# A decoder layer's MLP: third tile of right operands from another pool, and a seventh tile for sums

## The chip, the cores and the metric

The kernel runs on one core of one Trainium2 chip. The metric is the device time of one execution in microseconds; before the change the median of three runs is 2434.29 us (2431.82 to 2435.8). The core has five engines, which work at the same time, each through its own list of instructions in a fixed order: PE (TensorE: matmuls, with PEld for its weight loads), DVE (VectorE), ACT (ScalarE), POOL (GpSimd) and SP (SyncE), which here issues the DMAs. An instruction waits until what it reads is written and what it overwrites is no longer needed; everything behind it on the same engine waits with it.

## The reference

One layer of a decoder on 2048 tokens of width 1024: stick-breaking attention in 12 heads beside a cross-attention of 4 heads into 256 memory tokens, one output projection, a layer norm, and an MLP with a squared ReLU and a second layer norm.

```python
proj = x @ w_in_sb[slot]
mix = merge_heads(stick_breaking_attention(q, k, v))
mem_out = memory_attention(q_mem, mem, w_mem_kv[layer])
y = jnp.concatenate([mix, mem_out.astype(mix.dtype)], axis=-1) @ w_out[layer]
x = layer_norm(DN_ALPHA * x + y, ln_mix_g[layer], ln_mix_b[layer])
h = jnp.square(jax.nn.relu(x @ w_up[layer]))
x = layer_norm(DN_ALPHA * x + h @ w_down[layer], ln_ffn_g[layer], ln_ffn_b[layer])
```

All inputs are float32. `w_up` is 1024 x 4096, `w_down` 4096 x 1024.

## The kernel before

Each float32 operand of a matmul is split into two float16 parts, a high part (ACT writes it) and a low part (DVE writes the difference: `split_sb`, lines 713 and 714, for operands in SBUF; `split_ps`, lines 161 and 162, for those in PSUM). A product is three passes over these parts: high by high, high by low, low by high (`PASSES`). The first two passes need the high part of the left factor of `matmul`, `lhsT`, and only the last needs its low part.

The projections and the attention come first, until about 1090 us. Their order on every engine is written out by hand. There `turn` (lines 313 to 319) splits each block of attention weights into a tile of the pool "p2" (ACT line 317, POOL line 318), and SP issues a DMA that transposes it (line 319). A tile of "p2" can be written again when that DMA has read it. The pool has six tiles.

Then comes the MLP, in two halves of 1024 tokens. It multiplies by a scheme of Strassen's kind: seven products of blocks where eight would be needed, on sums and differences of blocks. The 4096 columns of `w_up` are taken in 16 blocks of columns, `fp` = 0 to 15, in pairs (`GROUP` = 2). For one block, `up` (from line 812) makes seven products of 12 matmuls each, in three banks of PSUM, `upa`, `upb` and `upc`: r11 into `upa`, rt2 into `upb`, rt1 into `upc`, r21 into `upa`, rt3 into `upb`, r22 into `upc`, rt4 into `upb`. The banks are read by ACT and DVE in between: `u1` is a copy of `upa` by ACT (line 863), DVE adds it to `upb` (line 866) and to `upc` (line 869), and later lines 874, 876 and 878 add further products. A product that goes into a bank for the second time waits for the instruction that reads the first. Lines 836 to 841 apply the squared ReLU and split the result into seven tiles `hl`, and `sums` (lines 843 to 856) makes four sums of them. After the two blocks of a pair, `down` (from line 891) multiplies the `hl` by the rows of `w_down`, in the tiles `wr`, in banks `dna`, `dnb` and `dnc`, and adds to `acc` (DVE lines 917, 919, 948 and 956, POOL lines 921 and 958). The last pair (`fp` 14 and 15) takes plain products in `down`.

The right operands of one block of `up` are seven split matrices, in four tiles: keys 0 to 2 hold two each (r11 and rt2; rt1 and r21; rt3 and rt4) and key 3 holds r22. In half 0 they are made from `w_up`: SP loads two raw tiles `wu` (line 788, pool "st", three tiles), POOL makes four differences `t` (line 774, in tiles of "p2"), ACT and DVE split, and SP stores the split tiles to DRAM (`keptup`, line 768). The rows of `w_down` go the same way: raw tiles `wd` (line 889, "st"), differences `t_d` (line 774, "p2"), splits into `wr`, stores `keptdown`. In half 1 the stored tiles are loaded again (line 816 for `rt`, line 1135 for `wr`).

Pools are lists of equal tiles under a tag. "X" has 16 tiles of 4 KB per partition. In the MLP eight of them hold `acc` and seven hold `hl`. "ws" has five tiles of 4 KB, "p2" six of 2 KB, "st" three. In the MLP the order of instructions on each engine is set by a scheduler when the kernel is built, from its own estimate of times and from which tile is free when; it is fixed at run time.

Of the kernel before, what the change touches and what calls it, by code (L numbers as in the profile page):

```python
# [10 lines left out]
F16 = mybir.dt.float16  # L11
# [5 lines left out]
P = 128  # L17
# [17 lines left out]
def trunk_layer(ctx: ExitStack, tc: tile.TileContext, x, mem, w_in, w_kv, w_out,  # L35
# [19 lines left out]
    HB = KT // 2  # L55
# [14 lines left out]


    DMA_DIAG = (2, 3)
    BUFS = dict(X=16, g=15, st=3, ws=5, et=7, p2=6, tt=2, pw=4)

    def sbt(tag, shape, dt, name):
        return sb.tile(shape, dt, tag=tag, name=name, bufs=BUFS[tag])

    def pst(tag, name):
        return pools["ps"].tile([P, C], F32, tag=tag, name=name, bufs=pools["bufs"][tag])
# [631 lines left out]
    def split_sb(hi, lo, src, scale):  # L711
        with early():
            A.activation(hi, src, AF.Copy, scale=scale)  # L713
            V.scalar_tensor_tensor(lo, src, scale, hi, ALU.mult, ALU.subtract)  # L714
# [44 lines left out]
    def operand(tiles, s, j, k):  # L759

        return tiles[s][j][:, :, k, :] if isinstance(tiles[s], list) else tiles[s][:, :, j * HB + k, :]
# [3 lines left out]
    def keep(key, t, shape):  # L765

        kept[key] = dr.tile(shape, F16, name="kept" + "_".join(map(str, key)))
        nc.sync.dma_start(kept[key], t)

    def right_sums(b11, b12, b21, b22, view, name):  # L770

        def diff(x, y, n):
            t = view(sbt("p2", [P, C], F32, f"t{n}_{name}"))
            G.tensor_tensor(t, x, y, ALU.subtract)
            return t

        t1 = diff(b12, b11, 1)
        t2 = diff(b22, t1, 2)
        t3 = diff(b22, b12, 3)
        t4 = diff(b21, t2, 4)  # L780
        return t1, t2, t3, t4

    def up_right(fp, nm):

        raw = []
        for i in range(2):
            t = sbt("st", [P, HB, 2 * P], F32, f"wu{nm}_{i}")
            nc.sync.dma_start(t, w_up[i * HB * P:(i + 1) * HB * P, fp * 2 * P:(fp + 1) * 2 * P]
                              .rearrange("(k p) f -> p k f", p=P))
            raw.append(t)  # L790
        b11, b12 = raw[0][:, :, :P], raw[0][:, :, P:]
        b21, b22 = raw[1][:, :, :P], raw[1][:, :, P:]
        t1, t2, t3, t4 = right_sums(b11, b12, b21, b22, lambda t: t.rearrange("p (k f) -> p k f", f=P), nm)

        def right(key, *srcs):
            n = len(srcs)
            t = sbt("ws" if n == 2 else "p2", [P, n, 2, HB, P], F16, f"rt{nm}")
            for i, s in enumerate(srcs):
                split_sb(t[:, i, 0], t[:, i, 1], s, SW)
            keep(("up", fp, key), t, [P, n, 2, HB, P])  # L800
            return [t[:, i] for i in range(n)]

        r11, rt2 = right(0, b11, t2)
        rt1, r21 = right(1, t1, b21)
        rt3, rt4 = right(2, t3, t4)
        r22, = right(3, b22)
        return r11, rt2, rt1, r21, rt3, rt4, r22

    def up(half, fp, ops, hl, wr, g, plain):


        nm = f"{half}_{fp}"
        if half:
            def right(i, n):
                t = sbt("ws" if n == 2 else "p2", [P, n, 2, HB, P], F16, f"rt{nm}")
                nc.sync.dma_start(t, kept["up", fp, i])
                return [t[:, i] for i in range(n)]

            r11, rt2 = right(0, 2)
            rt1, r21 = right(1, 2)  # L820
            rt3, rt4 = right(2, 2)
            r22, = right(3, 1)
        else:
            r11, rt2, rt1, r21, rt3, rt4, r22 = up_right(fp, nm)
        def prod(bank, s, r, start):
            bv = bank.rearrange("p (t n) -> p t n", n=P)
            n = 0
            for a, b in PASSES:
                for k in range(HB):
                    T.matmul(bv, lhsT=r[:, a, k, :], rhs=operand(ops, s, b, k), start=start and n == 0,  # L830
                             stop=n == 3 * HB - 1, skip_group_check=not start)
                    n += 1

        def activate(t, s, src=None):

            A.activation(t, t if src is None else src, AF.Relu, scale=math.sqrt(SH) / (SX * SW))  # L836
            if s is not None:
                A.activation(hl[s][:, g, 0, :], t, AF.Square)
            A.activation(t, t, AF.Square)
            if s is not None:  # L840
                V.tensor_tensor(hl[s][:, g, 1, :], t, hl[s][:, g, 0, :], ALU.subtract)  # L841

        def put(s, t):
            split_sb(hl[s][:, g, 0, :], hl[s][:, g, 1, :], t, 1.0)

        def sums(h11, h12, h21, h22):
            s1 = sbt("et", [P, C], F32, f"s1_{nm}")
            V.tensor_tensor(s1, h21, h22, ALU.add)
            put(S1, s1)
            s2 = sbt("et", [P, C], F32, f"s2_{nm}")  # L850
            V.tensor_tensor(s2, s1, h11, ALU.subtract)
            put(S2, s2)
            V.tensor_tensor(h21, h11, h21, ALU.subtract)
            put(S3, h21)
            V.tensor_tensor(h12, h12, s2, ALU.subtract)
            put(S4, h12)

        ba = pst("bk", f"upa{nm}")
        bb = pst("bk", f"upb{nm}")
        bc = pst("bk", f"upc{nm}")  # L860
        prod(ba, A11, r11, True)
        u1 = sbt("et", [P, C], F32, f"u1_{nm}")
        A.activation(u1, ba, AF.Copy)  # L863
        prod(bb, S2, rt2, True)
        u2 = sbt("et", [P, C], F32, f"u2_{nm}")
        V.tensor_tensor(u2, bb, u1, ALU.add)
        prod(bc, S1, rt1, True)
        u3 = sbt("et", [P, C], F32, f"u3_{nm}")
        V.tensor_tensor(u3, bc, u1, ALU.add)  # L869
        prod(ba, A12, r21, False)  # L870
        h11 = sbt("et", [P, C], F32, f"r_{nm}")
        activate(h11, A11, ba)
        prod(bb, S3, rt3, False)
        V.tensor_tensor(u3, bb, u3, ALU.add)  # L874
        prod(bc, S4, r22, False)
        V.tensor_tensor(u2, bc, u2, ALU.add)
        prod(bb, A22, rt4, False)
        V.tensor_tensor(u1, bb, u1, ALU.add)
        activate(u3, A22)
        activate(u1, A21 if plain else None)  # L880
        activate(u2, A12)
        if not plain:
            sums(h11, u2, u1, u3)
        if half:
            return
        rows = []
        for f in range(2 * fp, 2 * fp + 2):
            t = sbt("st", [P, D], F32, f"wd{nm}_{f}")
            nc.sync.dma_start(t, w_down[f * P:(f + 1) * P, :])
            rows.append(t)  # L890
        b11, b12, b21, b22 = (r[:, n * C:(n + 1) * C] for r in rows for n in range(2))
        ts = (b12,) if plain else right_sums(b11, b12, b21, b22, lambda t: t, "d" + nm)
        for s, t in zip((B11, B21, B22, T1, T2, T3, T4), (b11, b21, b22) + ts):
            split_sb(wr[s][:, g, 0, :], wr[s][:, g, 1, :], t, SD)
            keep(("down", fp, s), wr[s][:, g], [P, 2, C])
# [125 lines left out]
    for c in range(NC):  # L1021
        if c < len(kv_work):
            fn, hp, c0, nm = kv_work[c]
# [100 lines left out]
    for half in range(NC // 2):  # L1124
        if half == 0:
            load_gb(g2, b2, [(gbs[:, 0], gbs[:, 1]), (gbs[:, 2], gbs[:, 3])])
        for f0 in range(0, NFP, GROUP):
# [21 lines left out]
            for n, _ in enumerate(work):  # L1149
                i = n // 2  # L1150
# [38 lines left out]
```

## Time and profile before

| what | us |
|---|---|
| median of three runs | 2434.29 |
| the profiled execution | 2430.05 |
| its span, from first to last instruction | 2428.3 |
| PE busy in the span | 2237.2 |
| DVE busy | 1709.7 |
| ACT busy | 1185.7 |
| POOL busy | 1021.7 |

A row of the timeline gives start, length, engine, source line, operation, what is written, what is read (buffer numbers are left out), and the count of instructions merged into it; square brackets hold the idle time ahead of it and what ended it. A row of the windows gives the stretch, its length and the busy time and count of each engine, then the granted clock of PE as a share of full speed, the share of the DMA engines and GB/s. A row of the chain gives start, length and what the end of the stretch was waiting for at that time. A row of the waits gives who waited for whom, the total, the count and the longest.

### The profile page before, as it was taken

The numbers are of one execution on the slowest core, as the hardware profiler recorded it, in microseconds if no ns is written. First come the engines' busy times: TensorE is split into PE (matmuls) and PEld (weight loads), VectorE is DVE, ScalarE is ACT, GpSimd is POOL, SyncE is SP. The second block draws the span as 40 slices with busy tenths as digits, with TensorE's granted clock in tenths as the row PEclk, the third lists the DMA queues.
The fourth block names the chain that finished last, engine by engine and source line by source line (L and its number), as shares of the span: only waits on it lengthen the run. The fifth ranks groups of instructions, "written<-read, shape, count | busy, mean of one in ns | idle before, by whom it ended". The sixth has DMA issues, their size and how long they took to land.

```text
span 2428.3 us, 34523 instructions
## 1 busy us (share of the span) xinstructions
PE 2237.2 (92%) x12032; PEld 1000.8 (41%) x12032; DVE 1709.7 (70%) x2385; ACT 1185.7 (49%) x2577; POOL 1021.7 (42%) x826
## 2 busy tenths in 40 slices
PE   7798999999989999997799999999997999999996
PEld 4343434344334343333344444444443444444443
DVE  4456777777776777779987888888676454555447
ACT  4456677776766656544544454445433322233321
POOL 0001656566564556564654456443443122211124
PEclk9899999999999999998999999999998999999998
DMA  7244888879887787876643445334565333323211
GB/s 260 44 85 90 154 162 152 162 137 163 150 160 143 165 173 170 167 178 183 220 165 114 142 152 182 133 115 149 169 194 190 105 109 96 108 87 96 96 44 70
DMA packets 606285, 342.03 MB, mean 141 GB/s; under 512 B 487840, under 2 KB 544672, under 8 KB 606112
## 3 DMA queue, kind: packets, MB, share of 16 engines
q1 hardware_dynamic: 606112, 339.84, 55.8%
q8 instruction: 94, 1.54, 0.3%
q14 instruction: 79, 0.65, 0.1%
HBM read 143.65 MB, written 77.59 MB: 91 GB/s over the span
## 4 chain that ended last, share of the span: by engine, by line
PE 58%; DVE 18%; issue 8%; ACT 7%; DMA 5%; POOL 3%; SPq 0%; ACTq 0%; DVEq 0%; POOLq 0%
PE dnb L906 7%; PE upb L830 7%; PE dnc L906 5%; PE dna L906 5%; PE upc L830 5%; PE upa L830 4%; PE pq L252 4%; PE z L280 4%; PE op L670 4%; PE av L340 3%; PE kp L252 3%; PE vp L252 3%; DVE wr L714 2%; DVE e L466 2%; POOL t L318 2%
## 5 line engine op out<-in xcount | busy, mean ns | idle before, releaser
L318 POOL TENSOR_TENSOR t<-e,t 128x512 f16<-128x512 f32 (+1 forms) x384 | 431.6, 1150 | 360.0 <-ACT t L317 293.0
L830 PEld LDWEIGHTS <-rt 128*128 128x128 f16 x2688 | 266.2, 99 | 387.7 <-issue 81.1
L906 PEld LDWEIGHTS <-hl 128*128 128x128 f16 x2736 | 267.4, 98 | 335.5 <-DVE hl L841 11.2
L466 DVE TENSOR_TENSOR_SCAN e<-z,carry,zero 128x512 f32<-128x512 f32 x288 | 350.4, 1265 | 44.5 <-ACT z L458 30.2
L921 POOL TENSOR_TENSOR acc<-acc,v 128x512 f32<-128x512 f32 x112 | 149.9, 1341 | 503.1 <-DVE acc L919 432.4
L458 ACT ACTIVATE z<-z 128x512 f32<-128x512 f32 (+1 forms) x480 | 226.6, 513 | 229.5 <-PE z L280 123.7
L830 PE MATMUL upb<-op,rt 128*128 128x512 f16 x1152 | 269.6, 383 | 13.0 <-DVE u L874 6.9
L906 PE MATMUL dnb<-wr,hl 128*128 128x512 f16 x1008 | 236.1, 380 | 0.0
L317 ACT ACTIVATE t<-e 128x512 f16<-128x512 f32 (+1 forms) x384 | 225.9, 616 | 7.7 <-DMA w<-t 6.9
L280 PE MATMUL z<-k,q 64*128 64x512 f16 (+3 forms) x1440 | 186.0, 349 | 32.3 <-DVE e L466 31.7
L830 PE MATMUL upa<-op,rt 128*128 128x512 f16 x768 | 184.8, 389 | 26.3 <-ACT u L863 19.3
L830 PE MATMUL upc<-op,rt 128*128 128x512 f16 x768 | 183.7, 387 | 16.1 <-DVE u L869 16.1
L670 PE MATMUL op<-wo,mx 128*128 128x512 f16 x720 | 171.6, 387 | 1.8 <-DVE acc L677 1.8
L466 DVE TENSOR_TENSOR_SCAN e<-z,zero 128x128 f32<-128x128 f32 (+1 forms) x192 | 147.0, 806 | 32.1 <-ACT z L458 24.9
L906 PE MATMUL dna<-wr,hl 128*128 128x512 f16 x672 | 155.0, 380 | 9.7 <-DVE hl L841 9.7
L906 PE MATMUL dnc<-wr,hl 128*128 128x512 f16 x672 | 161.1, 379 | 1.8 <-ACT hl L713 1.1
L340 PE MATMUL av<-w,v 128*64 128x512 f16 (+3 forms) x1440 | 145.9, 349 | 4.5 <-DMA w<-t 4.5
L252 PE MATMUL vp<-xT,wv 128*128 128x512 f16 x576 | 140.4, 388 | 0.0
L252 PE MATMUL pq<-xT,wq 128*128 128x512 f16 x576 | 138.7, 385 | 0.0
L252 PE MATMUL kp<-xT,wk 128*128 128x512 f16 x576 | 136.0, 380 | 0.0
L836 ACT ACTIVATE u<-u 128x512 f32<-128x512 f32 x96 | 60.3, 628 | 132.9 <-DVE u L874 78.6
L280 PEld LDWEIGHTS <-q 64*128 64x128 f16 x1440 | 55.4, 94 | 148.7 <-issue 104.7
(177 smaller groups left out, 3248.0 us busy)
## 6 DMA issues: line engine op xcount, KB each, us to landing
keptdown<-wr SPq DMA_DIRECT2D x106, 256.0 KB, 2.5
wr<-keptdown SPq DMA_DIRECT2D x106, 256.0 KB, 2.9
keptup<-rt SPq DMA_DIRECT2D x48, 512.0 KB, 3.0
rt<-keptup SPq DMA_DIRECT2D x48, 512.0 KB, 3.6
wu<-in_w_up_dram SPq DMA_DIRECT2D x32, 512.0 KB, 4.6
wd<-in_w_down_dram SPq DMA_DIRECT2D x32, 512.0 KB, 4.0
x<-in_x_dram SPq DMA_DIRECT2D x16, 512.0 KB, 10.3
acc<-in_x_dram SPq DMA_DIRECT2D x16, 512.0 KB, 5.2
```

The source lines that it names most:

```text
L252: T.matmul(pp, lhsT=wt[:, a, k, :], rhs=xs(xT, c, b, k), start=n == 0, stop=n == 3 * KT - 1)
L280: T.matmul(banks[h], lhsT=q[rows, a, i * P:(i + 1) * P], rhs=keys(b)[rows], start=n == 0, stop=stop and n == 2)
L317: A.activation(hi, src, AF.Copy)
L318: G.tensor_tensor(lo, src, hi, ALU.subtract)
L340: T.matmul(av[h * HD:(h + 1) * HD, i0 * P:].rearrange("p (t n) -> p t n", n=P), lhsT=vv(h, a), rhs=pT(h, b)[:, i0:, :], start=first and n ...
L458: A.activation(t.z[:, :t.W], t.z[:, :t.W], AF.Sigmoid, scale=-SCORE)
L466: V.tensor_tensor_scan(t.e[:, t.W - 1::-1], t.z[:, t.W - 1::-1], zero[:, 0:1].broadcast_to([P, t.W]), init, ALU.mult, ALU.add)
L670: T.matmul(pp, lhsT=lhs, rhs=W[f"o{k}"][:, kb, n * C:(n + 1) * C], start=m == 0, stop=m == 3 * NKO - 1)
L830: T.matmul(bv, lhsT=r[:, a, k, :], rhs=operand(ops, s, b, k), start=start and n == 0, stop=n == 3 * HB - 1, skip_group_check=not start)
L836: A.activation(t, t if src is None else src, AF.Relu, scale=math.sqrt(SH) / (SX * SW))
L906: mm = T.matmul(bank, lhsT=hl[s][:, g, a, i * P:(i + 1) * P], rhs=wr[r][:, g, b, :], start=start and m == 0, stop=m == 3 * n - 1, skip_gro ...
L921: G.tensor_tensor(sl, sl, u, ALU.add)
```

## The change

The tile of key 2 (rt3 and rt4) is no longer taken from "ws" but from "X", in both halves, and "p2" gets a seventh tile. So a block takes two of the five tiles of "ws", not three, and one of "X". No instruction is added or removed.

```diff
-    BUFS = dict(X=16, g=15, st=3, ws=5, et=7, p2=6, tt=2, pw=4)
+    BUFS = dict(X=16, g=15, st=3, ws=5, et=7, p2=7, tt=2, pw=4)
...
         def right(key, *srcs):
             n = len(srcs)
-            t = sbt("ws" if n == 2 else "p2", [P, n, 2, HB, P], F16, f"rt{nm}")
+            t = sbt(("ws", "ws", "X", "p2")[key], [P, n, 2, HB, P], F16, f"rt{nm}")
...
             def right(i, n):
-                t = sbt("ws" if n == 2 else "p2", [P, n, 2, HB, P], F16, f"rt{nm}")
+                t = sbt(("ws", "ws", "X", "p2")[i], [P, n, 2, HB, P], F16, f"rt{nm}")
                 nc.sync.dma_start(t, kept["up", fp, i])
```

In the attention every engine keeps its order. In the MLP the scheduler sets another, the same for each pair of blocks but the first and the last. The three pieces below are from half 0, around blocks 4 and 5; a name like rt_5_14491 is a tile with the number of its block and its own number (14477, 14484, 14491 and 14498 are keys 0 to 3 of block 5).

POOL, beside the `down` of the pair before (L921 and L958 add to `acc`); t_0_5 are the differences for block 5, t_d_4 those for the rows of `w_down`:

```order
 L774 TENSOR_TENSOR t_d_4_14435<-wd_4_9_14427,t_d_4_14431 128x512
 L774 TENSOR_TENSOR t_0_5_14469<-wu_5_0_14465 128x512
+L774 TENSOR_TENSOR t_0_5_14471<-wu_5_1_14467,t_0_5_14469 128x512
 L921 TENSOR_TENSOR acc_9441<-acc_9441,v_0_0_14055 128x512
+L774 TENSOR_TENSOR t_0_5_14473<-wu_5_1_14467,wu_5_0_14465 128x512
 L921 TENSOR_TENSOR acc_9921<-acc_9921,v_0_1_14064 128x512
 L958 TENSOR_TENSOR acc_10616<-acc_10616,v_0_0_14088 128x512
```

Two differences of block 5 move up past eight additions to `acc`.

DVE, in block 4 from the first reading of `upb` (L866) to that of `upc` (L869):

```order
 L866 TENSOR_TENSOR u_0_4_14329<-upb_4_14301,u_0_4_14315 128x512
-L714 SCALAR_TENSOR_TENSOR rt_5_14498<-wu_5_1_14467,rt_5_14498 128x512
-L714 SCALAR_TENSOR_TENSOR rt_5_14491<-t_0_5_14473,rt_5_14491 128x512
-L714 SCALAR_TENSOR_TENSOR rt_5_14491<-t_0_5_14475,rt_5_14491 128x512
+L714 SCALAR_TENSOR_TENSOR rt_6_14926<-wu_6_0_14914,rt_6_14926 128x512
 L714 SCALAR_TENSOR_TENSOR wr_4_3_14258<-t_d_5_14632,wr_4_3_14258 128x512
 L919 TENSOR_TENSOR acc_11077<-acc_11077,dnb_2_14164 128x512
+L714 SCALAR_TENSOR_TENSOR wr_4_4_14259<-t_d_5_14634,wr_4_4_14259 128x512
 L919 TENSOR_TENSOR acc_11286<-acc_11286,dnb_3_14173 128x512
-L714 SCALAR_TENSOR_TENSOR wr_4_4_14259<-t_d_5_14634,wr_4_4_14259 128x512
+L714 SCALAR_TENSOR_TENSOR wr_4_5_14260<-t_d_5_14636,wr_4_5_14260 128x512
+L869 TENSOR_TENSOR u_0_4_14343<-upc_4_14302,u_0_4_14315 128x512
```

L869 stood behind eight instructions after L866 (the eighth, a split of wr_4_6, follows this piece, and L869 after it) and now stands behind six; the splits of key 2 of block 5 have left this place.

ACT, in block 4 from the end of `u2` (L839 on u_0_4_14329) to the copy of block 5's `upa` (L863):

```order
 L839 ACTIVATE u_0_4_14329<-u_0_4_14329 128x512
-L713 ACTIVATE rt_6_14933<-t_0_6_14918 128x512
-L713 ACTIVATE rt_6_14933<-wu_6_1_14916 128x512
+L713 ACTIVATE rt_7_15129<-wu_7_0_15117 128x512
 L836 ACTIVATE u_0_4_14315<-u_0_4_14315 128x512
 L839 ACTIVATE u_0_4_14315<-u_0_4_14315 128x512
-L713 ACTIVATE rt_6_14940<-t_0_6_14922 128x512
-L713 ACTIVATE rt_6_14940<-t_0_6_14924 128x512
 L713 ACTIVATE hl_4_3_14251<-s_0_4_14411 128x512
 L863 ACTIVATE u_0_5_14518<-upa_5_14503 128x512
```

Four splits of block 6 leave this place, and one of block 7, which reads a raw tile two blocks ahead, comes in front of L836. On DVE the same split stands in front of L848, and the splits of key 2 of block 5 now come behind the four sums of block 4, those of block 6 behind the last product of block 5. On SP the load of that raw tile, wu_7_0, stands behind the stores of keys 0 and 3 of block 6 in both kernels.

In half 1 the first load of a key-2 tile after the first, rt_1_18632, stands behind the eight loads of `acc` for the second half, and PE takes the two products of that tile, rt3 and rt4 of block 1, in one row of 24 matmuls behind five products of `down`. In later pairs the load of the odd block's key 2 stands behind the load of key 1 of the block two further.

## Rows read from the trace of the kernel before

**Rows 1.** Windows: attention, one pair of blocks in half 0, half 1.
```profile
225.00:1090.00 865.00, 809.15 (x5195) 342.02 (x5196) 658.62 (x773) 560.89 (x1416) 508.81 (x447) 0.99 0.82 159
1363.00:1442.00 79.00, 73.27 (x338) 32.92 (x337) 66.86 (x85) 37.29 (x65) 39.86 (x28) 1.00 0.42 147
1865.00:2428.00 563.00, 545.04 (x2526) 246.88 (x2524) 297.33 (x484) 159.27 (x262) 131.50 (x102) 0.99 0.29 91
```

**Rows 2.** Waits of PE from 1245 to 1700 us.
```profile
PE upc L830 <- DVE u L869: 15.7, 6, 2.9
PE upb L830 <- DVE u L866: 4.7, 5, 1.0
PE upb L830 <- DVE u L874: 4.7, 3, 1.6
PE upa L830 <- ACT u L863: 3.5, 5, 0.7
```

**Rows 3.** Timeline of PE, one pair of blocks.
```profile
1416.51 0.59 PE L830 MATMUL upa<-op,rt 128*128 128x512 f16 x2
1419.62 2.75 PE L830 MATMUL upc<-op,rt 128*128 128x512 f16 x12 [2.52 <-DVE u L869]
...
1426.31 5.12 PE L830 MATMUL upb<-op,rt 128*128 128x512 f16 x23 [1.57 <-DVE u L874]
...
1436.02 2.75 PE L830 MATMUL upa<-op,rt 128*128 128x512 f16 x12 [0.69 <-ACT u L863]
...
1441.23 2.75 PE L830 MATMUL upb<-op,rt 128*128 128x512 f16 x12 [0.95 <-DVE u L866]
```

**Rows 4.** Timeline of PE, waits in three other places.
```profile
1195.39 4.63 PE L830 MATMUL upa<-op,rt 128*128 128x512 f16 x12 [10.96 <-ACT u L863]
...
1498.52 4.25 PE L830 MATMUL upc<-op,rt 128*128 128x512 f16 x12 [2.52 <-DVE u L869]
...
1656.63 4.41 PE L830 MATMUL upc<-op,rt 128*128 128x512 f16 x12 [2.52 <-DVE u L869]
```

**Rows 5.** Chain of waits from 1395 to 1420 us.
```profile
1397.28 1.75 DVE wr L714 x2
...
1401.04 1.28 POOL t L774
...
1402.34 3.99 DMA wd<-in_w_down_dram
...
1406.88 1.13 ACT wr L713 x2
...
1418.89 0.68 DVE u L869
```

**Rows 6.** Timeline of DVE from 1409 to 1426 us.
```profile
1409.53 0.68 DVE L866 TENSOR_TENSOR u<-upb,u 128x512 f32<-128x512 f32 x1
...
1412.63 1.75 DVE L714 SCALAR_TENSOR_TENSOR wr<-t_d,wr 128x512 f16<-128x512 f32 x1
1414.31 1.27 DVE L919 TENSOR_TENSOR acc<-acc,dnb 128x512 f32<-128x512 f32 x2
1415.50 3.46 DVE L714 SCALAR_TENSOR_TENSOR wr<-t_d,wr 128x512 f16<-128x512 f32 x2
...
1425.58 0.68 DVE L874 TENSOR_TENSOR u<-upb,u 128x512 f32<-128x512 f32 x1
```

**Rows 7.** Instructions on tile u: durations in ns, least, median, most.
```profile
L836 ACT ACTIVATE u<-u x33: 613/630/631, 1287.4 to 1687.5; 128x512 f32<-128x512 f32 x33
...
L848 DVE TENSOR_TENSOR s<-u,u x11: 692/693/1525, 1295.6 to 1688.9; 128x512 f32<-128x512 f32 x11
...
L863 ACT ACTIVATE u<-upa x10: 573/576/580, 1329.0 to 1671.7; 128x512 f32<-128x512 f32 x10
```

**Rows 8.** Loads of wu (line 788): issue of one, and landing.
```profile
L788 SPq DMA_DIRECT2D wu<-in_w_up_dram x32: 383/386/1005, 1090.8 to 1706.7; - x32
...
DMA to landing us min/median/max: 3.9/4.6/5.6
```

**Rows 9.** Loads of rt in half 1 (line 816): landing.
```profile
DMA to landing us min/median/max: 2.5/3.6/10.9
```

**Rows 10.** Waits of ACT in the attention.
```profile
ACT t L317 <- DMA w<-t: 6.9, 8, 2.0
```

## What the change was predicted to do, and why

> **What bounds the kernel now.** I read the busy times by window first, to see which engine fills each part. In half 1 PE is busy 545 of 563 us [rows 1]: nothing that only moves other engines' work can gain much there. In the attention PE is busy 809 of 865 us and the list of instructions stays the same. Half 0 of the MLP is the place to look: a pair of blocks takes 79 us, in which PE works 73 and DVE 67 [rows 1], so PE sets the pace with holes in it.
>
> The waits of PE come next. From 1245 to 1700 us, which is six pairs, it waits 15.7 us for L869, 4.7 for L866, 4.7 for L874 and 3.5 for L863 [rows 2], together 28.6. The timeline of one pair shows where: 2.52, 1.57, 0.69 and 0.95 us, 5.73 in the pair [rows 3]. In three of the later pairs there is no wait for L874, but the 12 matmuls behind the wait for L869 take 4.25 us (first) to 4.41 (last) instead of 2.75 [rows 3, 4]. That is about 1.6 us three times, 4.8 in all. So the repeated loss is 28.6 + 4.8 = 33.4 us over six pairs. The first pair has a hole of its own, 10.96 us at the copy L863 [rows 4].
>
> Why L869 is late is read from the chain of waits: a split of `wr` on DVE frees a tile, POOL makes a difference (1.28), only then can the next raw rows be loaded (3.99), ACT splits (1.13), and the chain ends at 1418.89 with L869 [rows 5]. On DVE the instructions between L866 and L869 are slow ones: a split of two SBUF operands takes 1.75 us there, or 3.46 for two, where one that reads PSUM takes 0.64 to 0.68 [rows 6].
>
> **The change part by part.** Nothing is added or removed, so busy time changes only by what lies beside what. "X" has 8 + 7 of 16 tiles in use, so there is one tile for key 2, and its next use must wait until `up` has read it and its store has gone. "ws" now holds keys 0 and 1 of two and a half blocks instead of all three of one and two thirds.
>
> *Wait for L869.* Two differences of block 5 are made earlier on POOL, so the raw tile is free earlier and the load of `wd` starts earlier. Three splits of key 2 leave the stretch in front of L869 and a single new one comes: six instructions instead of eight. Two DVE splits fewer are worth 1.4 us at 0.68 each (the least row) to 3.5 (the pair in [rows 6]); with the load no longer last, L869 begins at 1418.89 less about 3.3 to 5.4, at 1413.5 to 1415.6. PE is ready at 1416.51 + 0.59 = 1417.10 [rows 3]. The wait of 2.52 goes, and with it the slow matmuls behind it.
>
> *Wait for L874.* With that wait gone PE comes to its next wait at 1426.31 − 1.57 − 2.52 = 1422.2, and L874 ends at 1426.26 now [rows 3, 6]. It would have to come forward by 4.0, and 3.3 to 5.4 is what L869 gives. So it is 0.7 late or has 1.4 to spare; I take it as just in time.
>
> *A new wait for L863.* This is the price. ACT's split of a raw tile of block 7 now stands ahead of L836 on `u1`, and DVE's half of it ahead of L848. Everything behind waits with them: the squared ReLU, the sums, the `hl`, and the copy L863, which lets PE write `upa` again. The raw tile is loaded by SP only behind the stores of keys 0 and 3 of block 6, so the load can't start before the splits of block 6 are done. From the end of L874 the chain is: three activations of `u2` and `hl` at 0.63, 1.9 us [rows 7]; two DVE instructions at 0.68, 1.4 [rows 6]; two issues by SP at 0.386, 0.8, and the load, 4.6 [rows 8]; ACT's split, half of 1.13 [rows 5], 0.6; L836 and L839 at 0.63, 1.3; L848, 0.7; the split of `hl` and L863 at 0.57, 1.1 [rows 5, 7]. Sum 12.4. PE meanwhile has work from 1426.26 to 1436.02 − 0.69 = 1435.33, which is 9.1 us [rows 3]. So PE would wait 3.3 us at `upa`. If L874 has its spare 0.7 or more this is 2.6; if L874 is 0.7 late, the sum of both waits is 4.0. With landings of 3.9 and 5.6 [rows 8] it moves by −0.7 and +1.0, and if the two DVE instructions are slowed to 1.75 each [rows 6] by another 2.1. The least that it can be is no wait, if the stores are issued before L874 ends. I take 3.3 (the median landing and the durations of undisturbed rows).
>
> *Wait for L866* (0.95 a pair) [rows 3]. Three fewer splits stand before it, at least 2 us: it goes. The splits of the odd block's key 2 now come behind the four sums of the even block; they are needed some 12 matmuls behind L866 and I count them as hidden by these.
>
> So of 5.6 us lost per pair 3.3 stays: 33.4 − 6 × 3.3 = 13.6 us gained.
>
> *First pair.* Two splits of key 2 fewer stand ahead of the copy that ends the hole of 10.96 [rows 4]: two ACT splits at 0.6 and as much on DVE. I take 2 us gained (0 to 5).
>
> *The seventh tile in the attention.* ACT line 317 waits 6.9 us in eight places for the transposing DMA to free a tile [rows 10]. With a tile more these waits go. How much of it reaches PE, which works 809 of 865 us [rows 1], the trace doesn't show; 0 to 6.9, and I take 1.5, nearer the low end since these waits are short and PE has other work in the list then.
>
> *Start of half 1.* The two products of block 1's key 2 now stand in a row in `upb`, so the second must wait for L874, one DVE instruction, 0.7 us, and the sums behind it come late: L878, L836, L839, L848 and a split of `hl`, some 3.3 us at the durations of [rows 6, 7], less three matmuls. I take 3.3 lost (0 to 6). *Half 1 after that.* The key-2 tile of an odd block is loaded behind its predecessor's last reading; 44 matmuls, 2.75 for 12 [rows 3], are about 10 us of cover, against 0.4 of issue, a landing of 3.6 [rows 9] and the load that is ahead of it. Hidden at the median; with the longest landing, 10.9, it would be some 2.3 us late in each of six pairs.
>
> **The sum.** 13.6 + 2 + 1.5 − 3.3 = 13.8. The profiled execution took 2430.05 us, its span 2428.3 and 1.75 around it. 2430.05 − 13.8 = 2416.2; the median of the runs is 4.2 above the profiled execution, so about 2420 as a median.
>
> **The skill against the trace.** Pure waits of the same size that repeat in every pair are in [rows 2, 3]. The Trainium skill, "Perfetto Trace Analysis", section "Optimization Strategy", says of such consistent bubbles that they can mean that there is not enough room for the next tile. By that rule a tile more would close them all, which is the first rival below. The trace agrees only in part, since the chain in [rows 5] goes through a tile that POOL waits for, but also through a load and the order on DVE. Against the change speaks "SBUF — State Buffer", section "Who interferes with whom": a DVE instruction with two SBUF inputs and a GpSimd instruction that reads SBUF hold each other up. The trace agrees: 1.75 against 0.68 [rows 6]. By it the two differences that move up on POOL would slow DVE's splits around `down`; the time would be that of the third rival.
>
> **The rivals.** Let r be what a pair still loses; then the gain is 33.4 − 6r + 0.2.
>
> *All repeated waits go.* The load of block 7's raw tile is there in time, because its stores come forward with everything else, and only a wait like the 0.69 of today stays. For it: SP has few issues in a pair and the DMA engines are busy 0.42 [rows 1]. Against it: the load is ordered behind stores of splits that are made only just before. r = 0.7, gain 29.4, 2405.
>
> *Nothing changes.* The new wait is as large as the old ones. r = 5.5, from the landing of 5.6 and half of the slowing on DVE, gain 0.6: 2434. Likewise if the load in half 1 is late (13.8 less 6 × 2.3 is 0).
>
> *Slower: ACT held up by the load.* The split of the raw tile two blocks ahead stands in front of L836 on ACT and L848 on DVE. The landing takes 5.6 and both DVE instructions 1.75, so the wait is 3.3 + 1.0 + 2.1 = 6.4, with L874 late by 0.7, r = 7.1, loss 9.0: 2443. It decides from r = 5.6 on. For it: one engine in order behind a load is what makes L869 late today. Against it: all the costs must be at their high ends at once, in every pair.
>
> **How the numbers follow.** Forecast 0.54, all waits gone 0.17, nothing 0.15, slower 0.14. What a measurement of this kernel can tell from no change is 0.2%, 4.9 us; the first two cases are faster by more, so faster 0.71, same 0.15, slower 0.14. The range goes from 2403, the better rival with the attention's share at 3, to 2440, which takes in the case of no change and part of the slower one. The forecast's own range, r from 2.6 to 4.3, is 2416 to 2427.
>
> **What would show it.** Right: PE's waits for L869 and L866 gone in half 0, pairs of 75 to 77 us instead of 79; ACT line 713 on `rt` waiting for a load of `wu` ahead of L836, and PE's wait for L863 grown to about 3 us a pair; no waits of ACT line 317 for the transposing DMA; the first hole shorter than 10.96; a wait at `upb` at the start of half 1. Wrong: PE still waiting for L869, so that the number of instructions ahead of it was not its cause; a wait for L863 under 1 us or over 5; or PE in half 1 waiting for a load of `rt`.

## The result and the profile after

The changed kernel takes 2457.97 us (median of 4 runs, 2454.59 to 2462.73), the kernel before 2434.44: 23.5 us slower. The ratio estimated from the runs is 1.013, with a 95% interval of [1.0098, 1.0163]; it is not the quotient of these two medians, which is 1.0097. The forecast was 2420, 14 us faster, and its range ended at 2440.

The profiled execution has a span of 2452.8 us, 24.5 more than before. It is cut at two places that both kernels have: the first product of half 0, and the wait of `upa` for L863 in the first pair of half 1. A third place, the first product of half 1, parts the stretch between them. PE's timeline before:

```profile
1148.92 5.28 PE L830 MATMUL upa<-op,rt 128*128 128x512 f16 x12 [4.11 <-DVE op L162]
...
1805.85 1.02 PE L830 MATMUL upa<-op,rt 128*128 128x512 f16 x4 [2.81 <-ACT op L161]
...
1841.11 1.03 PE L906 MATMUL dna<-wr,hl 128*128 128x512 f16 x2 [9.24 <-DVE hl L841]
...
1850.05 4.22 PE L830 MATMUL upa<-op,rt 128*128 128x512 f16 x12 [4.17 <-ACT u L863]
```

and after:

```profile
1150.62 4.64 PE L830 MATMUL upa<-op,rt 128*128 128x512 f16 x12 [3.43 <-DVE op L162]
...
1828.85 1.02 PE L830 MATMUL upa<-op,rt 128*128 128x512 f16 x4 [2.48 <-ACT op L161]
```

The second place after is 1860.54, the first row under "Start of half 1" below. So what comes before the MLP gave +1.7, half 0 with the start of half 1 709.9 instead of 701.1 (+8.8), the rest 592.3 instead of 578.3 (+14.0). The sum is 24.5. The +8.8 hide something: up to the first product of half 1 it is 678.2 instead of 656.9, so half 0 lost 21.3; from there to the second place it is 31.7 instead of 44.2, 12.5 won. There the kernel before has the wait of 9.24 shown above, and the changed one doesn't.

**Half 0.** PE's waits from 1245 to 1720 us of the changed kernel; the columns are those of [rows 2]:

```profile
PE upa L830 <- ACT u L863: 20.4, 6, 4.2
PE upb L830 <- DVE u L874: 11.3, 6, 2.6
PE upc L830 <- DVE u L869: 7.3, 5, 1.6
PE dnc L906 <- DVE acc L919: 3.5, 5, 0.7
```

The four are 42.5 us, where [rows 2] had 28.6. L866 is gone, L869 halved, L874 and L863 have grown. One pair on PE's timeline, which answers to [rows 3]:

```profile
1425.40 2.75 PE L830 MATMUL upc<-op,rt 128*128 128x512 f16 x12 [1.39 <-DVE u L869]
...
1432.27 5.34 PE L830 MATMUL upb<-op,rt 128*128 128x512 f16 x24 [1.75 <-DVE u L874]
...
1445.62 5.28 PE L830 MATMUL upa<-op,rt 128*128 128x512 f16 x12 [4.12 <-ACT u L863]
...
1473.94 2.75 PE L906 MATMUL dnc<-wr,hl 128*128 128x512 f16 x12 [0.69 <-DVE acc L919]
...
1509.48 2.75 PE L830 MATMUL upc<-op,rt 128*128 128x512 f16 x12 [1.50 <-DVE u L869]
```

The pair takes 1509.48 − 1425.40 = 84.1 us (82.6 to 84.1 over four pairs; the pair before these takes about 80, with a wait for L863 of 0.48) instead of 78.9. Waits are 1.39 + 1.75 + 4.12 + 0.69 = 7.95, and the 12 matmuls behind the longest take 5.28 instead of 2.75. Windows of that place (the first behind the wait for L863, the second behind that for L874) give the granted clock as the third figure from the end:

```profile
1445.60:1449.00 3.40, 3.38 (x9) 1.18 (x9) 3.40 (x7) 2.68 (x5) 0.00 (x0) 0.50 0.02 5
...
1432.30:1437.40 5.10, 5.10 (x24) 2.32 (x24) 4.97 (x5) 4.10 (x7) 3.82 (x3) 1.00 0.86 328
```

After 4.12 us of idleness PE ran at 0.50, its lower level (1.2 GHz); after 1.75 us it kept 1.00. So here a wait of 4.1 us cost about 6.6 with the matmuls behind it; the other four such waits, 3.6 to 4.2 us, cost 4.9 to 5.7.

What PE waits for is in the chain of waits of the changed kernel, which ends with that `upa`:

```profile
1422.55 4.29 DMA wu<-in_w_up_dram
...
1426.87 0.64 ACT rt L713
...
1427.53 1.81 DVE rt L714
...
1431.62 0.60 DVE u L874
...
1437.30 0.32 SPq L768
...
1437.71 4.16 DMA wu<-in_w_up_dram
...
1441.89 0.63 ACT rt L713
1442.52 0.53 ACT u L836
...
1443.73 0.70 DVE s L848
...
1445.09 0.49 ACT u L863
```

Both late ends have the same form: a raw tile `wu` of a block two ahead is loaded, ACT and DVE split it, and only behind that, in their fixed order, stands what PE needs. ACT's waits from 1245 to 1700 us say the same for the whole stretch; in the kernel before this wait was 8.7 us in five places:

```profile
ACT rt L713 <- DMA wu<-in_w_up_dram: 81.4, 23, 4.4
```

**Start of half 1.** PE's timeline of the changed kernel:

```profile
1860.54 4.44 PE L830 MATMUL upa<-op,rt 128*128 128x512 f16 x12 [4.33 <-ACT u L863]
...
1867.28 2.75 PE L830 MATMUL upc<-op,rt 128*128 128x512 f16 x12 [0.80 <-DVE u L869]
...
1883.15 5.30 PE L830 MATMUL upb<-op,rt 128*128 128x512 f16 x12 [4.91 <-DMA rt<-keptup]
1889.23 2.75 PE L830 MATMUL upb<-op,rt 128*128 128x512 f16 x12 [0.78 <-DVE u L874]
1892.77 0.81 PE L906 MATMUL dnb<-wr,hl 128*128 128x512 f16 x3 [0.78 <-DVE u L878]
1895.48 1.89 PE L906 MATMUL dnc<-wr,hl 128*128 128x512 f16 x4 [1.91 <-ACT hl L713]
```

and the chain there:

```profile
1867.81 9.51 DMA out_dram<-acc
...
1877.34 5.77 DMA rt<-keptup
...
1883.15 5.32 PE upb L830 x12
```

The key-2 tile of block 1 takes the place in "X" of a finished row of half 0, so its load waits for that row's store (9.51), and lands 5.77 later. New waits 0.80 + 4.91 + 0.78 + 0.78 + 1.91 = 9.2, and 2.55 of slower matmuls: 11.7 of the 14.0. The later pairs of half 1 wait for no load.

### The profile page after: what moved, and what is told of

It reads as the page before. It is cut to its first block, busy times and chain, and to the rows that moved or that the text cites. A ratio compares the mean times of both kernels' runs of the same rounds, so it can differ in the third digit from the quotient of the medians.

```text
span 2452.8 us, 34452 instructions
## 1 busy us (share of the span) xinstructions
PE 2243.7 (91%) x12032; PEld 1001.4 (41%) x12032; DVE 1686.0 (69%) x2385; ACT 1184.7 (48%) x2577; POOL 1039.6 (42%) x826
## 4 chain that ended last, share of the span: by engine, by line
PE 51%; DVE 17%; DMA 10%; ACT 7%; issue 7%; POOL 6%; SPq 1%; ACTq 0%; POOLq 0%; DVEq 0%
PE upb L830 7%; PE dnb L906 5%; PE upa L830 4%; DMA wu<-in_w_up_dram 4%; PE upc L830 4%; PE dnc L906 4%; PE op L670 3%; PE av L340 3%; PE dna L906 3%; PE z L280 3%; PE pq L252 3%; PE kp L252 3%; PE vp L252 3%; DVE e L466 2%; DVE rt L714 2%
## 5 line engine op out<-in xcount | busy, mean ns | idle before, releaser
L921 POOL TENSOR_TENSOR acc<-acc,v 128x512 f32<-128x512 f32 x112 | 152.0, 1363 | 410.4 <-DVE acc L919 351.7
L830 PE MATMUL upa<-op,rt 128*128 128x512 f16 x768 | 193.3, 402 | 38.0 <-ACT u L863 31.4
L836 ACT ACTIVATE u<-u 128x512 f32<-128x512 f32 x96 | 60.1, 626 | 136.9 <-DVE u L874 88.3
L628 POOL TENSOR_TENSOR acc<-acc,gb 128x512 f32<-128x512 f32 x60 | 84.6, 1437 | 75.8 <-ACT acc L622 75.8
```

The lines of the kernel that those rows point to most:

```text
L628: G.tensor_tensor(sl, sl, gb["g", n], ALU.mult)
L921: G.tensor_tensor(sl, sl, u, ALU.add)
```

## The experiments

For each profile the table gives the median, the ratio to the kernel before with its interval, the time of one pair of half 0, all of half 0 up to the first product of half 1, the two parts as cut above, and whether L841 at the start of half 1 was held up, which is told with `before_vector`.

| run | median us | ratio | pair | half 0 | first part | second part | L841 held up |
|---|---|---|---|---|---|---|---|
| before | 2434.44 | | 78.9 | 656.9 | 701.1 | 578.3 | yes |
| after | 2457.97 | 1.013 [1.0098, 1.0163] | 82.6 to 84.1 | 678.2 | 709.9 | 592.3 | no |
| p2_alone | 2434.16 | 1.0005 [0.998, 1.0029] | 78.8 | 658.1 | 702.4 | 578.3 | yes |
| x_half0 | 2456.54 | 1.0082 [1.0052, 1.0112] | 82.7 to 84.1 | 681.6 | 725.8 | 578.3 | yes |
| x_half1 | 2436.98 | 1.0015 [0.9995, 1.0036] | 78.9 | 659.6 | 692.5 | 589.2 | no |
| hold_split | 2432.75 | 1.0015 [0.999, 1.004] | 77.6 to 77.9 | 654.7 | 699.1 | 583.4 | yes |
| hold_two | 2433.62 | 1.0025 [1.0002, 1.0047] | 77.4 to 79.9 | 655.3 | 687.0 | 593.0 | no |
| hold_all | 2434.86 | 1.0031 [1.0008, 1.0054] | 77.6 to 79.7 | 653.9 | 685.6 | 594.2 | no |
| hold_all_h0 | 2416.84 | 0.996 [0.9934, 0.9986] | 77.8 to 79.3 | 655.2 | 686.9 | 578.6 | no |
| spare_as_raw | 2467.25 | 1.0176 [1.0122, 1.023] | 84.4 to 85.2 | 701.9 | 733.6 | 578.6 | no |
| hold_h0 | 2424.13 | 0.9956 [0.9937, 0.9976] | 77.1 to 77.7 | 649.8 | 695.2 | 577.9 | yes |
| hold_all_early | 2427.49 | 0.9987 [0.9963, 1.001] | 77.2 to 79.4 | 655.9 | 700.2 | 578.2 | yes |
| before_vector | 2426.3 | 0.9991 [0.997, 1.0012] | 78.9 | 658.3 | 693.7 | 578.2 | no |
| hold_h0_vector | 2416.2 | 0.9939 [0.9924, 0.9955] | 77.0 to 77.7 | 656.1 | 691.5 | 578.5 | no |

The ratios are to runs of the kernel before taken beside each group of kernels, whose medians there were 2434.52 (`p2_alone` to `hold_split`), 2429.45 (`hold_two` to `spare_as_raw`) and 2431.47 (the last four). The columns behind the ratio are of one execution each.

**The parts of the change.** `p2_alone` has only `p2=7`; `x_half0` and `x_half1` put back `"ws" if n == 2 else "p2"` in the other half's `right`.

p2_alone: 

> Only the seventh tile for sums; key 2 stays in its old pool. Theory (the loss is the order that follows from the key-2 tile, in half 0 a split of a raw tile that waits for its load ahead of the squared ReLU, in half 1 a key-2 tile that waits for a store): this part costs nothing, 2431 to 2437, with PE's waits for L869, L874, L863 and L866 in half 0 as in the kernel before. Rival (the seventh tile lets GpSimd run ahead and collide with VectorE, and this is the loss): 2450 or more.

x_half0: 

> The new place of key 2 in half 0 alone, with seven tiles for sums; half 1 as before. Theory: the pairs of half 0 stay at 83 us with PE waiting 4 us a pair for L863 behind a load of wu, and half 1 is as before: about 10 us over before, 2444 (2440 to 2449). Rival (the loss of half 0 comes back by the end of the half, all of it is half 1): 2434.

x_half1: 

> The new place of key 2 in half 1 alone, with seven tiles for sums; half 0 takes key 2 from its old pool. Theory: half 0 has pairs of 79 us, and at the start of half 1 PE waits about 5 us for the load of block 1's key 2, which waits for a store of the finished rows, with 2.5 us of slower matmuls and some 3.5 us of small waits behind it: about 13 us over before, 2447 (2443 to 2451). Rival (half 1 costs nothing of its own, the 14 us there are the lag of half 0): 2434.

The seventh tile costs and gives nothing that can be told. Half 0 alone makes nearly the whole difference of the medians (2456.54, above the 2440 to 2449 expected, where three of its ten runs lie). Half 1 alone ends within the bound of no change: its second part loses 11, with PE's wait of 4.13 us for the load, but its first part is 8.6 shorter, since there L841 isn't held up. The expectation of 2447 had not allowed for that.

**The place of the splits.** `hold_split` moves one instruction per pair on ACT, with its half on DVE; SP and POOL keep their order.

```diff
+                if key == 0 and i == 0 and fp % 2 and fp > 2:
+                    tc.add_manual_dep(mm.ins, copies[fp - 2].ins.name, ISSUE, reason="behind the copy")
```

Here `mm` is ACT's split and `copies` holds the L863 of each block. 

> The changed kernel, with one instruction moved: in half 0 the first split of an odd block's raw tile (on ScalarE, and with it its half on VectorE) goes from in front of the squared ReLU of u1 to just behind the copy L863. SyncE and GpSimd keep their order. Theory: PE's 4 us a pair for L863 and the slower matmuls behind it go, the 1.4 and 1.75 us for L869 and L874 stay, pairs of 77 to 78 us, 2458 less 6 x 5.5, about 2425 (2420 to 2435). Rival 1 (the three raw tiles are the bound, so that the same load only holds up something else): pairs of 82 to 83, 2452 to 2460. Rival 2 (collisions of VectorE with GpSimd): the same, 2452 to 2460, with the wait still at L863.

A pair on PE's timeline of `hold_split` (its lines stand some five further down: L868 is L863, L874 is L869, L879 is L874):

```profile
1427.03 2.75 PE L835 MATMUL upc<-op,rt 128*128 128x512 f16 x12 [1.40 <-DVE u L874]
...
1433.81 5.34 PE L835 MATMUL upb<-op,rt 128*128 128x512 f16 x24 [1.65 <-DVE u L879]
...
1443.67 2.75 PE L835 MATMUL upa<-op,rt 128*128 128x512 f16 x12 [0.64 <-ACT u L868]
...
1504.59 2.75 PE L835 MATMUL upc<-op,rt 128*128 128x512 f16 x12 [1.41 <-DVE u L874]
```

The 4.12 became 0.64, the matmuls behind it are at full speed, the other two waits stayed, and the pair takes 77.6. One instruction out of the way of L836 is worth 25 us in the medians (2457.97 to 2432.75, beside 2434.44 and 2434.52 of the kernel before), and half 0 in the traces is 23.5 shorter (678.2 to 654.7). That is the theory's number for the pair; the median lies at the upper end of its range.

`hold_two` and `hold_all` move DVE's halves of further splits, by the same means: those of key 1 of an even block behind L874 (`hold_two`), and the first split of an even block behind L869 as well (`hold_all`).

```diff
+                if key == 0 and i == 0 and fp % 2 == 0 and fp > 2:
+                    tc.add_manual_dep(lm.ins, seconds[fp - 2].ins.name, ISSUE, reason="behind the copy's sum")
+                if key == 1 and fp % 2 == 0 and fp > 2:
+                    tc.add_manual_dep(lm.ins, thirds[fp - 2].ins.name, ISSUE, reason="behind the sum")
```

hold_two: 

> hold_split, and besides the VectorE halves of the splits of key 1 of an even block (one of them reads a raw tile two blocks ahead) go from in front of L874 to just behind it. Theory (each wait left in the pair is a split of a raw tile two blocks ahead, in order in front of what PE waits for): the 1.7 us for L874 go, the 1.4 for L869 stay, pairs of 77.6 come to 76, 2433 less 10, about 2423 (2418 to 2429). Rival (three raw tiles turn over no faster than this, so what leaves L874 comes back elsewhere): pairs of 77 to 78, 2430 to 2436.

hold_all: 

> hold_two, and besides the VectorE half of the first split of an even block's raw tile goes from in front of L869 to just behind it; the other engines keep the order of hold_two. Theory: the wait for L869 goes too, pairs of 74 to 75, about 2414 (2409 to 2422). Rival 1 (the raw tiles' turnover): pairs of 77 to 78, 2430 to 2436. Rival 2 (the wait for L869 is the rows of w_down and VectorE's splits at 1.75 us beside GpSimd, as in the kernel before): the wait for L869 stays at 1 us or more, 2420 to 2426.

hold_all_h0, with key 2 in "ws" in half 1: 

> hold_all with key 2 in its old pool in half 1. Theory (the new place costs 2 to 3 us in half 1, as the run with half 1 alone showed between its two bounds): 2 to 3 us under hold_all, about 2411. Rival (half 1 costs nothing, or less than can be told): the same as hold_all.

PE's waits of `hold_two` from 1245 to 1720 us (L870 is L863, L876 is L869, L881 is L874):

```profile
PE upa L837 <- ACT u L870: 14.2, 6, 2.6
PE upc L837 <- DVE u L876: 6.0, 5, 1.9
PE dnc L913 <- DVE acc L926: 3.8, 5, 0.8
PE upb L837 <- DVE u L881: 0.6, 1, 0.6
```

The wait for L874 went from 11.2 to 0.6 and came back at L863, 3.2 to 14.2, with slower matmuls behind it. The rival was right: the pair is not shorter, and half 0 is as in `hold_split`. Two more splits now stand between L874 and L876 and lengthen the chain to the copy; whether the three raw tiles or DVE's own time sets the floor isn't shown. In `hold_all` the split is gone from in front of L869, and the wait for it is 0.24 us once and 0.90 to 1.47 in the other four pairs. So its theory failed, and no rival came in full: the wait left is what the second expected, in part, with the splits of `wr` in front of it as in [rows 5, 6]; the median, 2434.86, and the pair are those of the first. The intervals of both kernels lie just above 1.

Half 1 was not expected so. `hold_all` and `hold_all_h0` differ in half 1's place of key 2 alone, and by 18 us in the median, 15.6 in the second part. So where PE comes early to the start of half 1, key 2 in "X" costs all of the 14 us seen after the change. The expectation of 2 to 3 us was drawn from `x_half1`, where the shorter first part hid it.

**The other use of the spare tile.** `spare_as_raw` is the kernel before with `wu` of the second rows in "X".

```diff
-            t = sbt("st", [P, HB, 2 * P], F32, f"wu{nm}_{i}")
+            t = sbt("X" if i else "st", [P, HB, 2 * P], F32, f"wu{nm}_{i}")
```

> The kernel before with the spare tile of the pool of the activations used for the second raw tile of each block of w_up in half 0, which leaves the three raw tiles to six loads of a pair instead of eight; key 2 stays in its old pool, six tiles for sums. If the turnover of raw tiles is what ends the waits in the pairs: pairs of 75 to 77 and 2410 to 2422. If what decides is only the place of a split that waits for its load in the order of ScalarE and VectorE: 2430 to 2445, by where such a split now stands.

It is the slowest of all. In each pair PE waits for a split itself:

```profile
1445.62 4.24 PE L830 MATMUL upa<-op,rt 128*128 128x512 f16 x12 [6.47 <-ACT rt L713]
```

More raw tiles did not shorten the pair under the order that came with them; the run changes tiles and order together, so it doesn't say what more raw tiles would give under another order. Both expected ranges were too low.

**Later runs.** `hold_h0` is `hold_split` with key 2 in "ws" in half 1. `hold_all_early` is `hold_all` with the tile of block 1's key 2 in half 1 taken before the tiles of `acc`. `before_vector` and `hold_h0_vector` put the additions L634 of half 0's rows on DVE.

```diff
                 if half > 0 and fp == 0:
+                    taken[1, 2] = fetch(half, 1, 2, 2)
                     for tb in range(2 * half * TB, 2 * (half + 1) * TB):
...
-                ln_apply(a, mv[:, j, 0:1], rs[:, j:j + 1], 2 if tb < NT // 2 else 1)
+                ln_apply(a, mv[:, j, 0:1], rs[:, j:j + 1], 0 if tb < NT // 2 else 1)
```

hold_h0: 

> hold_split with key 2 in its old pool in half 1. Theory: pairs of 77.6 us as in hold_split, against 79 in hold_all_h0, and no loss at the start of half 1: 9 us under hold_all_h0 where VectorE's L841 at the start of half 1 isn't held up by GpSimd (about 2408), the same as it (2417) where it is. Rival (the pairs' order is worth nothing, only half 1 counts): 2417 with L841 short.

hold_all_early: 

> hold_all with the key-2 tile of block 1 in half 1 taken and loaded ahead of the eight loads of acc, so that it takes the tile that block 0's key 2 leaves and waits for no store of finished rows. Theory: PE's wait of 5.9 us for that load and the slower matmuls behind it go, the small waits of 0.8, 0.8 and 1.9 us stay: 2435 less 8, about 2427 (2423 to 2431). Rival (the load stays behind block 0's last product, and comes as late): 2433 to 2437.

before_vector: 

> The kernel before with the last additions of the layer norm of half 0's rows (L634, 16 of them, in a row on GpSimd while half 1 starts) on VectorE instead. Theory (the 13.8 us of one L841 at the start of half 1, 0.7 elsewhere, is GpSimd's unbroken row holding VectorE off): no instruction of VectorE over 3 us there, PE's wait of 9.2 us for it goes, 10 to 13 us of additions come onto VectorE, partly ahead of L866: 2424 to 2432 against 2430 to 2434. Rival (L841 waits for something else, which the record doesn't show): L841 stays at 10 us or more.

hold_h0_vector: 

> hold_h0 with the additions L634 of half 0's rows on VectorE, as in before_vector. Theory: the hold-up of L841 can't come up, 2408 to 2414, at most 4 us over hold_h0's best runs. Rival (the additions on VectorE cost more than the hold-up): 2415 to 2420.

`before_vector` is about the wait of 9.24 us in the kernel before. DVE's timeline of before at the start of half 1, and POOL's at the same time:

```profile
1827.23 13.82 DVE L841 TENSOR_TENSOR hl<-r,hl 128x512 f16<-128x512 f32 x1 [8.69 <-ACT r L839]
```

```profile
1827.03 1.28 POOL L634 TENSOR_TENSOR acc<-acc,gb 128x512 f32<-128x512 f32 x1
1828.25 2.51 POOL L628 TENSOR_TENSOR acc<-acc,gb 128x512 f32<-128x512 f32 x2
1830.70 9.81 POOL L634 TENSOR_TENSOR acc<-acc,gb 128x512 f32<-128x512 f32 x8
```

The instruction that takes 0.7 us elsewhere is on record for 13.82, until POOL's unbroken row ends at 1840.51. In `hold_all_h0` the same one (there L850) started in the middle of such a row, 1.0 us into an L628, and was through at once. POOL's row and DVE's:

```profile
1824.96 2.96 POOL L628 TENSOR_TENSOR acc<-acc,gb 128x512 f32<-128x512 f32 x2
```

```profile
1825.93 0.86 DVE L850 TENSOR_TENSOR hl<-r,hl 128x512 f16<-128x512 f32 x1 [7.01 <-ACT r L848]
```

With the additions on DVE, POOL's row has ended when L841 starts, PE's wait of 9.24 is gone and the first part is 7.4 shorter; the price is a later L863 (5.60 instead of 4.17). The median came as expected, 2426.3, and the rival, by which L841 would have stayed at 10 us, failed. The ratio's interval holds 1, so a gain of that kernel isn't shown, but its ten runs lie within 2421.1 to 2429.5, where those of before beside it spread over 2414 to 2435.

`hold_all_early` shows no wait for the key-2 load and a second part of 578.2, as before the change. But its profile has L841 held up, so that PE comes late enough to hide the load in any case; the median, 2427.49 against 2434.86 for `hold_all`, is what the theory gave. `hold_split`, held up too and with this tile taken late, has a second part of 583.4, which speaks for the early place.

`hold_h0` and `hold_h0_vector` beat the kernel before and the changed one. `hold_h0` has L841 held up in its profile and came to 2424.13, outside the 2408 and the 2417 that were expected, though two of its ten runs lie at 2409; `hold_h0_vector`, without the hold-up, came to 2416.2, which its rival had expected (2415 to 2420). The best versions are `hold_all_h0`, `hold_h0` and `hold_h0_vector`, 0.4 to 0.6% faster than before; their intervals overlap. Only a part of this comes from half 0: it takes 655.2, 649.8 and 656.1 us in these three and 656.9 before. The profile of `hold_all_h0` has a span 11.8 us shorter than that of before; 12.5 are won at the start of half 1, where L841 isn't held up, 1.8 in half 0, and 2.5 are lost elsewhere. The kernel before has such short runs too: of the 25 beside the last four kernels, 6 lie at 2414.4 to 2421.9 and the other 19 at 2429.2 to 2435.4. That the 6 are those without the hold-up isn't shown, since one execution of a kernel is profiled; so how much of the gain is a rarer hold-up stays open.

## Why the prediction was wrong

*The direction.* The sum held that 5.6 us lost per pair would become 3.3. It became 7.8 to 8.1 of waits and 1.5 to 2.5 of slower matmuls, 9.3 to 10.5 in the pairs of 82.6 to 84.1 us. This failed at three terms, and the start of half 1 added a fourth. Two of the prediction's own signs of being wrong came: PE still waits for L869, and in half 1 it waits for a load of `rt`.

*Wait for L869.* "L869 begins at 1413.5 to 1415.6", so the wait of 2.52 would go. It stayed at 1.4 to 1.6. The count of instructions in front of it, six instead of eight, was right (of the three splits that leave, one is of key 3 and two are of key 2), but one of the six is a split of a raw tile that waits for its own load, and three are the slow splits of `wr` of [rows 6]. `hold_all` shows that without the raw split 0.9 to 1.5 are left in four of five pairs. Of the 3.3 to 5.4 by which L869 was to come forward, two splits fewer account for 1.4 to 3.5; the other 1.9, for the load, are not worked out from a row.

*Wait for L874.* It was taken as "just in time". It is 1.75, behind two splits of key 1 of block 6, one of which waits for the load issued at 1422.55. The prediction looked at one raw tile two blocks ahead, the one in front of L836; the same form stood in front of L874. `hold_two`, which moves both, shows that they were the cause.

*The new wait for L863.* The chain was foreseen link by link, with SP's store, a load of 4.6 (4.16 came) and the splits, and summed to 3.3. It is 3.6 to 4.2. `hold_split` shows that this one split carries it. What was missed is what the wait does to PE: PE was at 0.50 behind it in the stretch shown, and the 12 matmuls there take 1.3 to 2.5 us more per pair. The prediction had counted such slower matmuls as a loss of the kernel before [rows 4] and as part of the gain, and had not asked whether the new, longer wait would bring them back.

*The slower rival* named this mechanism and gave it r = 7.1 and 2443, against which it held that all costs had to be high at once. They didn't have to be: with a landing of 4.16, under the median, and two more splits of the same form, r is 9.3 to 10.5.

*Wait for L866* and *ACT's waits for the transposing DMA.* Both went, as forecast. No run shows the 1.5 us that the second was to give PE: the first product starts at 1150.62 instead of 1148.92, over all profiles between 1148.0 and 1157.4, and `p2_alone` shows no change.

*First pair.* Two us of gain were counted. The hole of 10.96 became 6.72, but waits of 2.83 and 2.43 came ahead of it (1.27 and 2.24 before). From the first product to the wait for L874 in the second pair it is 1270.57 − 1150.62 = 119.95 instead of 1268.31 − 1148.92 = 119.39: no gain.

*Start of half 1.* 3.3 (0 to 6) was forecast from the two products in a row. Those small waits came, 3.5. The larger part, 4.9 of wait and 2.55 of slower matmuls, has a cause that wasn't seen: the key-2 tile takes the place of a finished row, and so waits for a store. The prediction read the order on SP (behind eight loads of `acc`) and not what the tile itself waits for. `hold_all` against `hold_all_h0` gives this term as 15.6.

*The wait of 9.24 for L841* was in the profile before and was not read as part of the sum, since the change doesn't touch it. It went in the changed kernel's profile; without the 12.5 won there its span would have been 37 longer, not 24.5, so it hid a third of the loss. That was luck: no term of the sum stood for it.

## What to carry to other kernels

Taking a tile from a fuller pool doesn't only take a wait away: it lets the scheduler place work for later blocks earlier, and on an engine that runs in order each such instruction that waits for a load holds up everything behind it. Read the new order for every instruction that reads a freshly loaded tile and stands in front of something PE waits for, not for the first one alone. And ask of a tile in a shared pool whose place it takes, and what that one still waits for. Compare two profiles stretch by stretch: an event that comes in some executions only, like the hold-up of L841, can be larger than what is looked for.

## What the runs showed of the hardware

One DVE instruction with two operands in SBUF was on record for 13.8 us (0.7 elsewhere) beside an unbroken row of POOL instructions that read SBUF, in six of the fourteen profiles (13.05 to 13.84); in six others it passed in 0.7 to 0.9 within such a row, and in the two with the additions on DVE it came after the row. In all six where it was held it began during an L634, in all six where it passed during an L628, as the rows above show for two; whether that decides isn't shown. The Trainium skill, "SBUF — State Buffer", section "Who interferes with whom", calls the port pair that the two share "an exclusive lock"; the trace agrees that one can wait for the other, and adds that DVE can be held off by a whole row of POOL instructions, not by one alone.

In the pairs of half 0 of the changed kernel, slower matmuls stood behind each wait of 3.6 to 4.2 us (12 in 4.1 to 5.3 us instead of 2.75) and behind none of the five waits of 1.75; in the kernel before they stood behind three of the waits of 2.5 to 2.9 and not behind the others. So in these pairs several short waits were cheaper than one long one of the same sum.
